# Weight splits and running sums on VectorE instead of GpSimd, and another order of the recurrence

## The chip, the cores and the metric

The kernel runs on one core of one Trainium2 chip. A core has five engines that run their own instruction rows in order and meet at semaphores: TensorE (PE, matrix products; PEld is its weight load), VectorE (DVE), ScalarE (ACT), GpSimd (POOL) and SyncE (SP, which here only issues DMAs). Matrix products write to PSUM; all else lies in SBUF. The metric is the device time of one execution in microseconds (us).

## What is computed

A two-layer network on 512 latent and 256 context tokens of width 1024. Layer 0 mixes tokens by a gated linear recurrence (RG-LRU), layer 1 by attention with compressed keys (MLA); each layer ends in a SwiGLU feed-forward (FFN). Every half of a layer normalises, shifts and scales its input by a modulation that depends on the conditioning vector, and adds its result, gated, to the residual. The part that the change touches most, cut down:

```python
def _rglru_coeffs(xc, gw, gb, lam):
    r = sigmoid(_blockdiag(xc, gw[0]) + gb[0])
    ig = sigmoid(_blockdiag(xc, gw[1]) + gb[1])
    log_a = -RG_C * r * softplus(-lam)
    return exp(log_a), sqrt(-expm1(2.0 * log_a)) * (ig * xc)

def _rglru_mixer(h_ctx, h_lat, ...):
    g, u = split(h @ w_in, 2)            # latent and context
    u = _dwconv_centred(u, conv_w, conv_b)
    for d, reverse in enumerate((False, True)):
        a, b = _rglru_coeffs(u, gate_w[d], gate_b[d], lam[d])
        y[d] = _linear_scan(a, b, h0, reverse)
    return ((y[0] + y[1]) * gelu(g)) @ w_out

def _rmsnorm(x, g):
    return x * rsqrt(mean(x * x, axis=-1) + NORM_EPS) * g
```

## The kernel before, in words

The residual xT lies transposed in SBUF: 8 tiles (m or k, 0 to 7) of 128 channels by 768 tokens, context behind the 512 latents. All products are in fp32 precision, made of three products of split numbers: a high half (wh, hh, uh, mh) and a low half (wl, hl, ul, ml), `mm3`: high by high, high by low, low by high. So each weight tile is split on the chip. SP loads a raw buffer (two of them), ACT writes the high half (L108), and `Stream._low` writes the low half, raw minus high (L119), on the engine that `low_engine` names: GpSimd at first, VectorE from the boundary ahead of FFN 0 on (`st.low_engine = dve`, L1061), GpSimd again for FFN 0's last boundary, and in later stages as MLA and FFN 1 set it. A split is 128x1024 in most cases. `advance` writes the high half of a unit and leaves its low half pending; the low half is written by the next `advance` or `flush`, so on the engine that does it the split stands behind all that was given to that engine in between. Writing the last low half of a raw buffer releases it, and SP's next load goes out. Four split tiles are held at a time.

The recurrence has four blocks n of 256 channels, and the list STEPS sets the order of everything in it by hand. A step is a letter and digits: `g` and `u` are the two input products of a block (48 matmul instructions each), `c` its convolution (L895 on ACT, six L899 on DVE, then the split L904 on ACT and L905 on DVE), `t` and `T` a gate product with its tanh (L931 on ACT), `e` the decay (L941 and L951 on DVE, L948 to L950 on ACT), `q` a root (L1037), `s` the states (L956, scans L958 and L959 or L962, L964 on DVE), `G` a GELU (L970), `m` the gated states and their split (L985 to L988), `o` one output product (12 matmul instructions) with its residual (L767 on DVE), `a` a step of the modulation of later stages, and `w` hands back a used weight tile, which is where `advance` is called. Three PSUM tiles go round among the products. The first digit is the block, the last of an `o` is m. START sets the order of the stage ahead of it in the same way: `H` is a flush, `B` and `D` transposes of rows of constants, `p` a product of the first input unit, `n` and `l` the normalisation.

`residual` adds an output product to xT (L767), squares the new xT on ACT (L783) and adds the square to a running sum (L785), on GpSimd, 52 times in the kernel. The addition is put off: it is written behind the L767 of the next m. In `boundary`, which writes the last half of a stage's output products and interleaves the next stage's normalisation (L669 and L672 on DVE, L671 on ACT), `flush_acc()` writes it at once for every m from the one on at which the first half's normalisation begins.

Of the kernel before, what the change touches and what calls it, by code (L numbers as in the profile page):

```python
# [12 lines left out]
ALU = mybir.AluOpType  # L13
# [3 lines left out]
D = 1024  # L17
# [20 lines left out]
START = (  # L38
    "H h0 L1 S00 X S01 S02 Y B S03 E0 h1 n0 l0 n1 h2 D S10 H l1 S11 S12 p01 S13 p00 L2 p10 E1 p11 n2 "
    "l2 S20 p02 p12 C S21 n3 S22 S23 l3 p20 p21 E2 n4 p22 p31 p30 l4 p32 n5 L3 S30 l5 A S31 S32 S33 "  # L40
# [21 lines left out]
class Stream:  # L62
# [3 lines left out]
    def __init__(self, nc, raw_pool, w_pool):  # L66
        self.nc, self.raw_pool, self.w_pool = nc, raw_pool, w_pool
        self.loads, self.units = [], []
        self.loaded = self.split = self.base = 0
        self.raw, self.tiles, self.freed, self.pending = {}, {}, set(), []  # L70
        self.hold = 0
        self.more = {}
        self.low_engine = nc.gpsimd

# [71 lines left out]
def kernel(ctx, tc, x, c, ctx_in, c_ctx, ada_w, ada_b, norm_mix_g, norm_ffn_g, ffn_w_in,  # L146
# [3 lines left out]
    nc = tc.nc  # L150
    act, dve, pe = nc.scalar, nc.vector, nc.tensor
# [109 lines left out]
    st = Stream(nc, raw_pool, w_pool)  # L261
# [23 lines left out]
    def lru_gate_unit(n, d):  # L285
# [18 lines left out]
        "a g31 s311 w o20 o21 G30 o22 G31 w m3 w o23 o24 o25 o26 o27").split()  # L304

# [458 lines left out]
    def residual(m, ps, l, ch, group, stat):  # L764
# [5 lines left out]
        if stat:  # L770
# [5 lines left out]
            else:  # L776
# [7 lines left out]
                if not at_end:  # L784
                    accs.append(lambda: nc.gpsimd.tensor_tensor(acc[:, s], acc[:, s], sq, op=ALU.add))  # L785

# [349 lines left out]
    def ffn0(na, nb, nxt):  # L1136
        ga, gb = na.group, nb.group
        with ExitStack() as es:
# [163 lines left out]
            for c, (h0, nh, outs) in enumerate(s0_out):  # L1302
# [3 lines left out]
                if lastp:  # L1306
                    ada_until(1, 4)
                    for m in range(KT):
                        ps = out_tile(c, m, (ga,), range(nh))
                        residual(m, lambda s: ps[1], 0, 5, ga, True)  # L1310
                        if m == 0:
                            st.flush()
                    st.low_engine = nc.gpsimd

                    def last(m):
# [440 lines left out]
```

## Time and profile before

| | us |
|---|---|
| median of 3 runs | 1568.83 |
| lowest, highest | 1565.91, 1569.62 |
| the profiled execution | 1571.79 |
| its span in the trace | 1569.9 |

| engine | busy us | share of the span |
|---|---|---|
| PE | 1512.2 | 96% |
| DVE | 934.2 | 60% |
| ACT | 675.9 | 43% |
| POOL | 281.5 | 18% |

Stages in the span: the start to some 48 us, the recurrence to 340, the mixer's last half and the boundary to 376, FFN 0 to 893, its boundary to 915, MLA to 1182, FFN 1 behind it. A share of busy time is a mean over stages; what bounds a stage is read from its windows and from the waits in it.

### The profile page before, as it was taken

The numbers are of one execution on the slowest core, as the hardware profiler recorded it, in microseconds if no ns is written. First come the engines' busy times: TensorE is split into PE (matmuls) and PEld (weight loads), VectorE is DVE, ScalarE is ACT, GpSimd is POOL, SyncE is SP. The second block draws the span as 40 slices with busy tenths as digits, with TensorE's granted clock in tenths as the row PEclk, the third lists the DMA queues.
The fourth block names the chain that finished last, engine by engine and source line by source line (L and its number), as shares of the span: only waits on it lengthen the run. The fifth ranks groups of instructions, "written<-read, shape, count | busy, mean of one in ns | idle before, by whom it ended". The sixth has DMA issues, their size and how long they took to land.

```text
span 1569.9 us, 21629 instructions
## 1 busy us (share of the span) xinstructions
PE 1512.2 (96%) x8903; PEld 1321.4 (84%) x8903; DVE 934.2 (60%) x1397; ACT 675.9 (43%) x989; POOL 281.5 (18%) x261
## 2 busy tenths in 40 slices
PE   7999998979999999999999998999998999999998
PEld 5877876868878898999989887899998888888887
DVE  5766778686855657767587457666537543233234
ACT  5486555734423241433424343766644322232223
POOL 3223333242010101001010332111144100000002
PEclk9999999989999999999999999999999999999999
DMA  9434333131233334333242112110112433223222
GB/s 359 127 108 135 108 122 120 59 103 48 68 108 114 104 112 128 114 114 122 94 141 64 51 56 69 29 43 28 54 54 75 161 118 104 81 98 117 81 69 93
DMA packets 134995, 155.14 MB, mean 99 GB/s; under 512 B 6252, under 2 KB 112353, under 8 KB 134897
## 3 DMA queue, kind: packets, MB, share of 16 engines
q1 hardware_dynamic: 122272, 112.21, 22.3%
q0 software_dynamic: 12320, 41.02, 8.2%
q8 instruction: 70, 1.15, 0.3%
q10 hardware_dynamic: 304, 0.53, 0.1%
q14 instruction: 29, 0.23, 0.0%
HBM read 151.64 MB, written 2.10 MB: 98 GB/s over the span
## 4 chain that ended last, share of the span: by engine, by line
PE 82%; DVE 11%; ACT 4%; issue 1%; DMA 1%; SPq 0%; POOL 0%; DVEq 0%; ACTq 0%; POOLq 0%
PE f L791 14%; PE fo L1212 11%; PE x L1166 10%; PE fo L791 8%; PE z L1166 5%; PE lo L791 3%; PE s L1555 3%; PE ga L791 2%; PE wo L791 2%; PE y L1166 2%; PE o L1597 2%; PE p L791 2%; PE g L791 2%; DVE yc L899 1%; PE t L1573 1%
## 5 line engine op out<-in xcount | busy, mean ns | idle before, releaser
L108 ACT ACTIVATE wh<-raw 128x1024 fp32r<-128x1024 f32 (+3 forms) x247 | 208.5, 871 | 203.9 <-PE fo L1212 64.5
L119 POOL TENSOR_TENSOR wl<-raw,wh 128x1024 fp32r<-128x1024 f32 (+3 forms) x66 | 157.5, 2397 | 328.8 <-ACT wh L108 328.6
L119 DVE TENSOR_TENSOR wl<-raw,wh 128x1024 fp32r<-128x1024 f32 (+2 forms) x181 | 169.3, 948 | 11.8 <-ACT wh L108 11.8
L767 DVE SCALAR_TENSOR_TENSOR xT<-fo,mod,xT 128x512 f32<-128x512 f32 (+1 forms) x124 | 74.1, 626 | 129.8 <-PE fo L1212 66.2
L239 POOL DMA_DIRECT2D ada<-in_ada_w_dram x96 | 51.7, 539 | 465.3 <-PE psada L570 217.9
L791 PE MATMUL f<-hh,wh 128*128 128x512 f32 x320 | 124.7, 390 | 0.0
L791 PE MATMUL f<-hh,wl 128*128 128x512 f32 x320 | 124.5, 389 | 0.0
L791 PE MATMUL f<-hl,wh 128*128 128x512 f32 x320 | 124.5, 389 | 0.0
L785 POOL TENSOR_TENSOR acc<-acc,sq 128x256 f32<-128x256 f32 (+1 forms) x52 | 50.7, 975 | 374.1 <-ACT sq L783 371.9
L1212 PE MATMUL fo<-ah,wh 128*128 128x512 f32 (+1 forms) x352 | 98.3, 345 | 0.9 <-DVE g L1273 0.8
L1212 PE MATMUL fo<-al,wh 128*128 128x512 f32 (+1 forms) x352 | 95.8, 338 | 0.4 <-DVE al L1201 0.4
L1212 PE MATMUL fo<-ah,wl 128*128 128x512 f32 (+1 forms) x352 | 95.3, 337 | 0.0
L1109 DVE TENSOR_TENSOR sg<-sg,f 128x512 f32<-128x512 f32 x20 | 13.7, 687 | 116.4 <-ACT sg L1108 116.4
L1108 ACT ACTIVATE sg<-f 128x512 f32<-128x512 f32 x20 | 12.0, 599 | 148.3 <-PE f L791 148.3
L791 PE MATMUL fo<-ah,wh 128*128 128x512 f32 (+1 forms) x200 | 73.0, 365 | 0.0
L791 PE MATMUL fo<-ah,wl 128*128 128x512 f32 (+1 forms) x200 | 72.7, 364 | 0.0
L791 PE MATMUL fo<-al,wh 128*128 128x512 f32 (+1 forms) x200 | 72.7, 364 | 0.0
L791 PEld LDWEIGHTS f<-hh,wh 128*128 128x128 f32 x320 | 60.1, 188 | 13.2 <-issue 0.8
L791 PEld LDWEIGHTS f<-hh,wl 128*128 128x128 f32 x320 | 60.1, 188 | 12.6
L791 PEld LDWEIGHTS f<-hl,wh 128*128 128x128 f32 x320 | 60.1, 188 | 12.4
L1212 PEld LDWEIGHTS fo<-ah,wh 128*128 128x128 f32 x352 | 56.2, 188 | 12.8 <-issue 4.6
L1212 PEld LDWEIGHTS fo<-al,wh 128*128 128x128 f32 x352 | 56.2, 188 | 8.0 <-DVE al L1201 0.7
(490 smaller groups left out, 4023.3 us busy)
## 6 DMA issues: line engine op xcount, KB each, us to landing
raw<-in_ffn_w_in_dram SPq DMA_DIRECT2D x26, 1024.0 KB, 4.9
ada<-in_ada_w_dram POOLq DMA_DIRECT2D x96, 256.0 KB, 3.1
raw<-in_ffn_w_out_dram SPq DMA_DIRECT2D x19, 1024.0 KB, 4.9
raw<-in_ffn_w_in_dram SPq DMA_DIRECT2D x36, 512.0 KB, 4.7
ada<-in_ada_w_dram POOLq DMA_DIRECT2D x30, 512.0 KB, 4.4
ada<-in_ada_w_dram SPq DMA_DIRECT2D x32, 256.0 KB, 5.5
raw<-in_lru_w_in_dram SPq DMA_DIRECT2D x10, 512.0 KB, 5.3
raw<-in_lru_gate_w_dram SPq DMA_DIRECT2D x16, 256.0 KB, 3.2
```

What stands on the lines that cost most here:

```text
L108: nc.scalar.activation(dst(hi), src(self.raw[load]), AF.Copy)
L119: self.low_engine.tensor_tensor(dst(lo), src(self.raw[load]), dst(hi).bitcast(F32), op=ALU.subtract)
L239: eng.dma_start(t, ada_w[l, k * P:(k + 1) * P, c0:c0 + 512])
L767: dve.scalar_tensor_tensor(xT[:, m, s], ps(s) if callable(ps) else ps[:, s], mod[:, l, ch, v, m:m + 1], xT[:, m, s], op0=ALU.mult, op1=ALU ...
L785: accs.append(lambda: nc.gpsimd.tensor_tensor(acc[:, s], acc[:, s], sq, op=ALU.add))
L791: pe.matmul(ps[:, off + s.start:off + s.stop], a, b[:, s], start=first and i == 0, stop=last and i == 2)
L899: dve.scalar_tensor_tensor(y[:, s0:s1], ps[:, s0 + o:s1 + o], convw(tap, k), y[:, s0:s1], op0=ALU.mult, op1=ALU.add)
L1166: pe.matmul(ps, w[:, o:o + P], x[:, k0 + k, s], start=first and k == 0 and q == 0, stop=last and k == 3 and q == 2, skip_group_check=not f ...
L1212: pe.matmul(ps[v], w[:, o:o + P], x[:, k, s], start=k == 0 and q == 0, stop=k == nh - 1 and q == 2)
L1555: pe.matmul(ps[:, o:o + 384], x, y[:, k0:k1], start=j == 0, stop=j == 4)
L1573: pe.transpose(ps[:, j * P:(j + 1) * P], prs[h, b][:, j // 3, j % 3 * P:(j % 3 + 1) * P], ident)
L1597: pe.matmul(ps[:, :256], x[:, t % 4, hs], y[:, t, :], start=t == 0 and j == 0, stop=t == NT - 1 and j == 2)
```

## The change

It does four things. `low_engine` is VectorE from the start, and the line that set it to GpSimd ahead of FFN 0's last boundary is gone; MLA and FFN 1 set it as before. The addition in `residual` is on VectorE. START has one flush more and the two first products of p exchanged. STEPS has another order: c11 ahead of s011, o10 behind t201, and block 2's last output products (o20 to o27) between the last gates, decays and states of block 3. GpSimd is left with 27 of its 66 splits and none of its 52 additions.

```diff
--- before.py
+++ after.py
@@ -36,7 +36,7 @@
 ENTRY_AT = (12, 6)
 
 START = (
-    "H h0 L1 S00 X S01 S02 Y B S03 E0 h1 n0 l0 n1 h2 D S10 H l1 S11 S12 p01 S13 p00 L2 p10 E1 p11 n2 "
+    "H h0 L1 S00 X S01 S02 Y H B S03 E0 h1 n0 l0 n1 h2 D S10 H l1 S11 S12 p00 S13 p01 L2 p10 E1 p11 n2 "
     "l2 S20 p02 p12 C S21 n3 S22 S23 l3 p20 p21 E2 n4 p22 p31 p30 l4 p32 n5 L3 S30 l5 A S31 S32 S33 "
     "p41 E3 n6 p40 l6 p42 p52 p51 p61 n7 p50 l7 C p60 p70 h3 p71 p62 p72 H C").split()
 
@@ -70,7 +70,7 @@
         self.raw, self.tiles, self.freed, self.pending = {}, {}, set(), []
         self.hold = 0
         self.more = {}
-        self.low_engine = nc.gpsimd
+        self.low_engine = nc.vector
 
     def load(self, cols, emit):
         self.loads.append([cols, emit, 0])
@@ -295,13 +295,13 @@
 
     STEPS = (
         "g01 a t000 w G01 T000 t001 w e000 T001 a g10 e001 G10 a q000 s000 q001 a t011 t010 w s001 a T010 "
-        "e010 T011 e011 u10 q010 w a a s010 q011 c10 u11 w s011 a a w g11 c11 t100 w T100 m0 G11 w a a "
+        "e010 T011 e011 u10 q010 w a a s010 q011 c10 u11 w c11 s011 a a w g11 t100 w T100 m0 G11 w a a "
         "t101 e100 T101 e101 q101 g20 q100 G20 w a o00 t110 T110 t111 T111 w a a s101 s100 o01 o02 e111 "
         "o03 o04 o05 o06 q111 e110 w s111 o07 w a u20 c20 a a q110 s110 w w u21 c21 g21 m1 a a t200 G21 "
-        "T200 o10 w e200 t201 a o11 T201 o12 o13 e201 w q200 a q201 s201 w s200 a t210 T210 a t211 T211 "
+        "T200 w e200 t201 o10 a o11 T201 o12 o13 e201 w q200 a q201 s201 w s200 a t210 T210 a t211 T211 "
         "e211 w u30 e210 c30 q210 w o14 o15 q211 s210 a a s211 w u31 c31 o16 a w o17 a t301 t300 m2 T300 "
-        "e300 T301 e301 a t310 w T310 t311 a e310 a T311 e311 q300 q310 q311 g30 q301 s300 s310 s301 w w "
-        "a g31 s311 w o20 o21 G30 o22 G31 w m3 w o23 o24 o25 o26 o27").split()
+        "e300 T301 e301 a t310 w T310 t311 a e310 T311 o20 o21 a e311 q300 q310 o22 q311 w o23 g30 q301 s300 a "
+        "w s310 G30 w o24 s301 o25 g31 s311 G31 o26 w m3 o27 w").split()
 
     g_units[0][0], = std_units(lru_w_in[0], 0, P)
     u_units[0] = [std_units(lru_w_in[0], D + i * P, P)[0] for i in range(2)]
@@ -782,7 +782,7 @@
                     sq = sq[:, :s.stop - s.start]
                 act.activation(sq, xT[:, m, s], AF.Square)
                 if not at_end:
-                    accs.append(lambda: nc.gpsimd.tensor_tensor(acc[:, s], acc[:, s], sq, op=ALU.add))
+                    accs.append(lambda: dve.tensor_tensor(acc[:, s], acc[:, s], sq, op=ALU.add))
 
     def mm3(ps, wh, wl, xh, xl, parts, first, last, off=0):
 
@@ -1310,8 +1310,6 @@
                         residual(m, lambda s: ps[1], 0, 5, ga, True)
                         if m == 0:
                             st.flush()
-                    st.low_engine = nc.gpsimd
-
                     def last(m):
                         ps = out_tile(c, m, (gb,), range(nh))
                         residual(m, lambda s: ps[0], 0, 5, gb, True)
```

DVE around the first output product that reads the second output unit of block 1, o14 (lo_4_2297). yc is a convolution, ul the low half of its result, tg and b are parts of gates and decays, wl the low half of a weight unit; before:

```order
L941 SCALAR_TENSOR_TENSOR tg_2167<-tg_2167,yc_1786 128x768
L951 SCALAR_TENSOR_TENSOR tg_2152<-b_2272,tg_2152 128x768
L899 SCALAR_TENSOR_TENSOR yc_2277<-u_0_2221,cols_d,yc_2277 128x511 x2
L899 SCALAR_TENSOR_TENSOR yc_2277<-u_0_2221,cols_d,yc_2277 128x510
L899 SCALAR_TENSOR_TENSOR yc_2277<-u_0_2221,cols_d,yc_2277 128x255 x2
L899 SCALAR_TENSOR_TENSOR yc_2277<-u_0_2221,cols_d,yc_2277 128x254
L905 TENSOR_TENSOR ul_2286<-yc_2277,uh_2285 128x768
L767 SCALAR_TENSOR_TENSOR xT<-lo_4_2297,mod,xT 128x512
```

and now:

```order
L941 SCALAR_TENSOR_TENSOR tg_2167<-tg_2167,yc_1786 128x768
L951 SCALAR_TENSOR_TENSOR tg_2152<-b_2272,tg_2152 128x768
L899 SCALAR_TENSOR_TENSOR yc_2277<-u_0_2221,cols_d,yc_2277 128x511 x2
L899 SCALAR_TENSOR_TENSOR yc_2277<-u_0_2221,cols_d,yc_2277 128x510
L899 SCALAR_TENSOR_TENSOR yc_2277<-u_0_2221,cols_d,yc_2277 128x255 x2
L899 SCALAR_TENSOR_TENSOR yc_2277<-u_0_2221,cols_d,yc_2277 128x254
L905 TENSOR_TENSOR ul_2286<-yc_2277,uh_2285 128x768
L119 TENSOR_TENSOR wl_2219<-raw_2110,wh_2218 128x1024
L767 SCALAR_TENSOR_TENSOR xT<-lo_4_2297,mod,xT 128x512
```

The split wl_2219 stands between ul and the residual of lo_4; before it was on POOL's row.

DVE around block 3's last decay, ahead of the products g30 and g31, before:

```order
L941 SCALAR_TENSOR_TENSOR tg_2540<-tg_2540,yc_2402 128x768
L951 SCALAR_TENSOR_TENSOR tg_2480<-b_2544,tg_2480 128x768
L941 SCALAR_TENSOR_TENSOR tg_2589<-tg_2589,yc_2277 128x768
L951 SCALAR_TENSOR_TENSOR tg_2568<-b_2614,tg_2568 128x768
L941 SCALAR_TENSOR_TENSOR tg_2636<-tg_2636,yc_2402 128x768
L951 SCALAR_TENSOR_TENSOR tg_2604<-b_2640,tg_2604 128x768
L956 TENSOR_TENSOR tg_2495<-tg_2495,tg_2518 128x768
L958 SCALAR_TENSOR_TENSOR tg_2495<-a_2521,tg_2495 128x256
L959 SCALAR_TENSOR_TENSOR tg_2495<-a_2521,tg_2495 128x512
```

and now:

```order
L941 SCALAR_TENSOR_TENSOR tg_2589<-tg_2589,yc_2277 128x768
L951 SCALAR_TENSOR_TENSOR tg_2568<-b_2614,tg_2568 128x768
L767 SCALAR_TENSOR_TENSOR xT<-lo_0_2634,mod,xT 128x512
L767 SCALAR_TENSOR_TENSOR xT<-lo_0_2634,mod,xT 128x256
L767 SCALAR_TENSOR_TENSOR xT<-lo_1_2649,mod,xT 128x512
L767 SCALAR_TENSOR_TENSOR xT<-lo_1_2649,mod,xT 128x256
L941 SCALAR_TENSOR_TENSOR tg_2632<-tg_2632,yc_2402 128x768
L951 SCALAR_TENSOR_TENSOR tg_2604<-b_2670,tg_2604 128x768
L767 SCALAR_TENSOR_TENSOR xT<-lo_2_2677,mod,xT 128x512
L767 SCALAR_TENSOR_TENSOR xT<-lo_2_2677,mod,xT 128x256
L119 TENSOR_TENSOR wl_2574<-raw_2441,wh_2573 128x1024
L767 SCALAR_TENSOR_TENSOR xT<-lo_3_2699,mod,xT 128x512
```

Three output products stand among the decays, and the split wl_2574, which g30 reads, stands behind the decay of tg_2604 and the residual of lo_2.

DVE in the last half of the mixer, ahead of FFN 0 (sq is ACT's square, nt and hl are the normalised input), before:

```order
L669 SCALAR_TENSOR_TENSOR nt_2_512_3101<-xT,gm,R_f0a 128x256
L672 SCALAR_TENSOR_TENSOR hl_79<-nt_1_512_3086,mod,hh_78 128x256
L767 SCALAR_TENSOR_TENSOR xT<-lo_5_3105,mod,xT 128x512
L669 SCALAR_TENSOR_TENSOR nt_3_512_3116<-xT,gm,R_f0a 128x256
L672 SCALAR_TENSOR_TENSOR hl_79<-nt_2_512_3101,mod,hh_78 128x256
L767 SCALAR_TENSOR_TENSOR xT<-lo_6_3120,mod,xT 128x512
L669 SCALAR_TENSOR_TENSOR nt_4_512_3131<-xT,gm,R_f0a 128x256
L672 SCALAR_TENSOR_TENSOR hl_79<-nt_3_512_3116,mod,hh_78 128x256
L767 SCALAR_TENSOR_TENSOR xT<-lo_7_3135,mod,xT 128x512
```

and now:

```order
L767 SCALAR_TENSOR_TENSOR xT<-lo_3_3072,mod,xT 128x512
L785 TENSOR_TENSOR acc<-acc,sq_3080 128x512
L669 SCALAR_TENSOR_TENSOR nt_1_512_3086<-xT,gm,R_f0a 128x256
L672 SCALAR_TENSOR_TENSOR hl_79<-nt_0_512_3069,mod,hh_78 128x256
L767 SCALAR_TENSOR_TENSOR xT<-lo_4_3090,mod,xT 128x512
L785 TENSOR_TENSOR acc<-acc,sq_3098 128x512
L669 SCALAR_TENSOR_TENSOR nt_2_512_3101<-xT,gm,R_f0a 128x256
L672 SCALAR_TENSOR_TENSOR hl_79<-nt_1_512_3086,mod,hh_78 128x256
L767 SCALAR_TENSOR_TENSOR xT<-lo_5_3105,mod,xT 128x512
L785 TENSOR_TENSOR acc<-acc,sq_3113 128x512
L669 SCALAR_TENSOR_TENSOR nt_3_512_3116<-xT,gm,R_f0a 128x256
L672 SCALAR_TENSOR_TENSOR hl_79<-nt_2_512_3101,mod,hh_78 128x256
```

Each L767 is followed by the addition of its own square.

## Rows read from the trace of the kernel before

**Rows 1.** The page, part 1: busy us of each engine.

```profile
PE 1512.2 (96%) x8903; PEld 1321.4 (84%) x8903; DVE 934.2 (60%) x1397; ACT 675.9 (43%) x989; POOL 281.5 (18%) x261
```

**Rows 2.** Windows: busy us of each engine, instruction counts, PE's granted clock, DMA.

```profile
300.00:350.00 50.00, 41.58 (x238) 35.71 (x237) 38.39 (x47) 24.00 (x33) 21.72 (x13) 0.90 0.26 84
...
376.00:860.00 484.00, 482.74 (x2906) 438.60 (x2905) 325.31 (x526) 169.70 (x288) 41.42 (x77) 1.00 0.34 103
```

**Rows 3.** Waits of PE, 100 to 352 us: total, times, longest in us.

```profile
PE lo L791 <- DVE xT L767: 8.2, 1, 8.2
...
PE ga L791 <- DVE yc L899: 5.1, 1, 5.1
...
PE ga L791 <- ACT tg L931: 1.4, 1, 1.4
...
PE lo L791 <- ACT tg L931: 3.0, 1, 3.0
...
PE ga L791 <- ACT uh L904: 3.0, 1, 3.0
```

**Rows 4.** Windows, one stretch after the wait for L767.

```profile
326.20:332.20 6.00, 6.00 (x19) 5.13 (x20) 5.96 (x9) 3.07 (x4) 0.35 (x1) 0.50 0.01 3
```

**Rows 5.** Timeline of PE (start us, duration, instruction): the last gate's end.

```profile
293.30 0.51 PE L791 MATMUL ga<-ul,wh 128*128 128x512 f32 x2
293.65 0.53 PE L791 MATMUL ga<-uh,wl 128*128 128x512 f32 x2
```

**Rows 6.** Groups (xcount, busy us, mean ns, idle before), 48 to 352 us, and timeline rows.

```profile
L119 POOL TENSOR_TENSOR wl<-raw,wh 128x1024 fp32r<-128x1024 f32 x31 | 82.4, 2661 | 101.1 <-ACT wh L108 100.8
...
L964 DVE TENSOR_TENSOR tg<-tg,tg 128x768 f32<-128x768 f32 x8 | 18.4, 2297 | 0.3
...
108.71 2.53 POOL L119 TENSOR_TENSOR wl<-raw,wh 128x1024 fp32r<-128x1024 f32 x1
...
109.08 2.98 DVE L964 TENSOR_TENSOR tg<-tg,tg 128x768 f32<-128x768 f32 x1
...
261.81 0.96 DVE L964 TENSOR_TENSOR tg<-tg,tg 128x768 f32<-128x768 f32 x1
```

**Rows 7.** Timeline of DVE: a split with no neighbour on POOL.

```profile
366.45 1.22 DVE L119 TENSOR_TENSOR wl<-raw,wh 128x1024 fp32r<-128x1024 f32 x1
```

**Rows 8.** Timeline of all engines around block 3's first convolution, c30.

```profile
245.03 3.12 POOL L119 TENSOR_TENSOR wl<-raw,wh 128x1024 fp32r<-128x1024 f32 x1 [6.85 <-ACT wh L108]
...
248.23 0.99 ACT L895 ACTIVATE yc<-u,cols_d 128x768 f32<-128x768 f32 x1 [0.37 <-PE u L791]
...
249.25 3.75 DVE L899 SCALAR_TENSOR_TENSOR yc<-u,cols_d,yc 128x511 f32<-128x511 f32 x6 [0.30 <-ACT yc L895]
...
253.97 0.96 DVE L905 TENSOR_TENSOR ul<-yc,uh 128x768 fp32r<-128x768 f32 x1 [0.97 <-ACT uh L904]
```

**Rows 9.** Timeline of DVE: the last decay of block 3.

```profile
303.57 0.96 DVE L951 SCALAR_TENSOR_TENSOR tg<-b,tg 128x768 f32<-128x768 f32 x1 [3.08 <-ACT tg L950]
```

**Rows 10.** Timeline of DVE: diagonals in the start and ahead of FFN 0.

```profile
15.17 3.06 DVE L855 TENSOR_SCALAR dgx<-ident,rst 128x128 f32<-128x128 f32 x6
...
368.23 0.88 DVE L656 TENSOR_SCALAR dg_f0b<-ident,rst 128x128 f32<-128x128 f32 x4
```

**Rows 11.** Timeline of DVE and ACT in the boundary ahead of FFN 0.

```profile
342.14 0.48 DVE L767 SCALAR_TENSOR_TENSOR xT<-lo,mod,xT 128x256 f32<-128x256 f32 x1 [0.24 <-PE lo L791]
...
356.92 0.74 DVE L767 SCALAR_TENSOR_TENSOR xT<-lo,mod,xT 128x512 f32<-128x512 f32 x1
...
358.65 0.74 DVE L767 SCALAR_TENSOR_TENSOR xT<-lo,mod,xT 128x512 f32<-128x512 f32 x1
...
360.76 1.88 DVE L119 TENSOR_TENSOR wl<-raw,wh 128x1024 fp32r<-128x1024 f32 x1
...
357.75 0.63 ACT L783 ACTIVATE sq<-xT 128x512 f32<-128x512 f32 x1 [0.35 <-DVE xT L767]
```

**Rows 12.** Groups of DVE in the boundary after FFN 0, 890 to 915 us.

```profile
L672 DVE SCALAR_TENSOR_TENSOR hl<-nt,mod,hh 128x256 fp32r<-128x256 f32 x6 | 6.8, 1130 | 2.1 <-ACT hh L671 2.1
```

## The prediction, made blind

> **What bounds the kernel now.** I read the page first: TensorE (PE) is busy for 96% of the span [rows 1], so a change can gain only from the time in which PE stands still or runs at a low clock, and can lose wherever PE is made to wait. The windows by stage say where such time is [rows 2]: in 376 to 860, layer 0's feed-forward product, PE is busy 482.74 of 484.00 us, and what VectorE (DVE) and GpSimd (POOL) do there costs nothing. In 300 to 350, the end of the recurrence, it is busy 41.58 of 50.00. The waits of PE between 100 and 352 us name the releasers [rows 3]: 8.2 us for DVE's L767, 5.1 for DVE's convolution (L899), 3.0 and 1.4 for ScalarE's (ACT) gate tanh (L931), 3.0 for the high half of the convolved input (L904). That is 20.7 us. After a wait comes a stretch in which the granted clock is 0.50 of full speed, that is 1.2 GHz: 326.20 to 332.20 follows the 8.2 us wait [rows 4]. Pairs of products start 0.35 us apart at full speed (293.30 and 293.65, [rows 5]) and, over these 6.00 us with 19 products in them, about 0.63 apart, so a slow stretch loses some 0.45 of its length. I call these slow stretches the tail of a wait.
>
> **The splits, moved from POOL to DVE.** 31 weight splits fall in 48 to 352 us and take 2661 ns each on POOL [rows 6]; the same 128x1024 split on DVE takes 1.22 us at 366.45 [rows 7]. POOL also slows DVE: L964 takes 2.98 us at 109.08, beside the split that starts at 108.71, and 0.96 at 261.81 with none beside it; its eight have a mean of 2297 ns [rows 6]. The eight alone lose 8 x (2.30 - 0.96) = 10.7 us, and I estimate some 40 us for all of DVE's instructions in this stretch, from the same comparison form by form. 31 x 1.22 = 38 us of splits come in. So DVE's load stays about as it is, and what matters is where each split stands in its row.
>
> The Trainium skill ("GPSIMD Engine Reference", section "8. Key points") says that elementwise work is about twice as fast on VectorE and that GpSimd shares its SBUF interfaces with VectorE instructions that have two SBUF inputs. The trace agrees: 2661 against 1220 ns, and 2.98 against 0.96. By this rule alone the change would gain; that is the first rival below, whose time is worked out from rows.
>
> On POOL a split starts when ACT has written the high half; nothing else stands ahead of it but some DMA issues. DVE takes its instructions in order, and the low half of a unit is written at the next step that advances the weights, behind all that DVE was given in between. Where one of these waits for ACT or PE, the split waits, and PE stops at the third product of the unit, the first that reads the low half. The largest case: output unit o14. Before, POOL made its split at 245.03 [rows 8]. Now it stands behind block 3's convolution and its L905. PE ends the u product at about 248.23, when ACT starts on it, the convolution runs from 249.25 for 3.75 us, L905 starts at 253.97 and takes 0.96, and a split of 1.22 follows: 253.97 + 0.96 + 1.22 = 256.15 [rows 7, 8]. PE would have wanted it at 248.23 + 2 x 0.35 + some 0.1 for the start. So about 7.1 us are lost, and a tail that I take like the one in [rows 4], 0.45 x 6.0 = 2.7: together 9.8.
>
> The second: g30. Its split now stands behind L951 of e311 and two L767. Before, the last gate's products ended at 293.65 + 0.53 = 294.2 [rows 5], and that L951 at 303.57 + 0.96 = 304.5 [rows 9]: 10.3 us later. Now PE has four output products (o20 to o23, six pairs each, 6 x 0.35 = 2.1 us) and one step of the modulation (some 0.6) ahead of g30, 9.0 us, and reaches the low half at 9.7. The split is done at 10.3 + 0.75 + 0.48 + 1.22 = 12.7. That is 3.0 lost, and a tail of 0.45 x 3.4 = 1.5 (a short one: between nothing and 2.7): 4.5.
>
> Walking the rest of the recurrence the same way (durations of the rows, the new order of each engine), I get these further new waits, all estimates: t000, 1.25 (its low half waits for two splits); t100, 1.25 (a split behind the first states); u20, 0.8; g21, 2.4 (behind a convolution and a state); T201, 1.2 (its tanh behind a decay on ACT); t210, 2.6 (behind L767 and a decay); t301, 2.0 (what stays of the wait for the last convolution, which starts when o14's loss is over); the first product of the mixer's last half, 2.5. Their sum is 14.0. With the two large ones it is 28.3.
>
> **The reordered steps.** Convolution c11 ahead of states s011 takes away the wait for L904, 3.0. The later o10 lets PE go on where it waited 3.0 and 1.4 for L931. The wait of 5.1 for c31's convolution goes, since DVE is late with it by the slowed L962 and L964 ahead of it (its rest is the t301 above). The output products among block 3's last gates take the 8.2 us wait away: L767 is no longer queued up behind all states. That is all of [rows 3], 20.7, and four tails of about 3.4, 3.4, 4.7 and 6.0 us, 0.45 x 17.5 = 7.9. Sum: 28.6. So the recurrence comes out at 28.3 - 28.6, about -0.3: the two halves of the edit cancel. I bound it by -20 and +12: the first if only o14's wait appears with its tail (9.8 - 28.6), the second if three of the waits over 2 us get a long tail too and c31's wait stays.
>
> **The start** (POOL beside DVE): the six dgx of the first normalisation take 3.06 us at 15.17 beside a split, where four of the like take 0.88 at 368.23 without a neighbour [rows 10]: 3.06 - 6 x 0.22 = 1.7 goes, and as much again, as an estimate, where two L669 of the same chain meet a split at 23.8. Two splits on DVE take 2 x 1.22 = 2.4 back, some 0.5 of it beside other waits. I put -1.5, between -3 and 0. The order of p00 and p01 and the extra flush change nothing else.
>
> **The sums of squares, moved to DVE.** This is an addition ahead of nothing in the feed-forwards, but in the boundaries between stages DVE is what PE waits for. From the second product of the last half on, the addition stands right behind the same m's L767 and so waits for ACT's square of it. In the rows of before, L767 starts at 356.92 and the next at 358.65, 1.73 apart; the square starts at 357.75 and ends at 358.38 [rows 11]. So the addition can start 358.38 - 356.92 = 1.46 after its L767, takes about 0.65 (an L767 of the same size, 0.74, overlapped as its neighbours are), and then come the normalisation's two (L669, L672) at 0.4 each: 2.9 from L767 to L767. Six m of 2.9 - 1.7 are 7.2; the split that POOL slowed to 1.88 us at 360.76 [rows 11] runs at its 1.22, and its neighbours too, some -1.2: +6. In the half ahead of it L767 comes every 0.72 us (0.48 and an idle of 0.24, [rows 11]); with an addition of 0.48 DVE needs 0.96, 7 x 0.24 = 1.7, and two of the last splits, 2.4, now lie on it: +4. PE waits for the last of this chain, so all of it counts: +10, between +5 and +12. After it, FFN 0 is full and gives nothing back.
>
> From FFN 0 to MLA the same loop runs with a slower PE (some 2.7 us per m), and POOL's splits slow L672 there to a mean of 1130 ns [rows 12], where an L767 of its size takes 0.48 [rows 11]; that goes: six m of 2.9, splits of 2 x 1.22 + 2 x 0.69 and a rest of 2 are 23.5 against 21 before: +3 with the start (0 to +5). From MLA to FFN 1, in halves of 256, the splits stay on POOL, and each of eight m gains a wait of about 0.3 and an addition of 0.48, 6.2 in all, less what L672 gets back when POOL's additions are gone, eight times up to 0.65 (the excess in [rows 12]), of which I take 4.2: +2 (0 to +4). At the end of FFN 1 PE needs as long for an m as DVE would: 0.
>
> **Sum.** -1.5 - 0.3 + 10 + 3 + 2 = +13.2 us. The profiled execution took 1571.8 us, 3.0 above the median of 1568.8; on its frame the sum gives 1585.0, on the median's 1582.0, which I take.
>
> **Rivals.** *Faster: POOL's neighbourhood was the real brake.* If DVE's freed time (40 us) comes at the instants where a split is due, the new waits stay at o14's alone: 9.8 - 28.6 = -19 in the recurrence, -3 at the start, and boundaries at their low end, +5: -17, or 1552. For it: DVE is free for 11.6 of the 50 us of 300 to 350 [rows 2], and L962 and L964 stand in the way of c31 and of the last L767. Against it: the splits' places behind waiting instructions are fixed by the order. It decides from a recurrence better by 13 us on. *No change*: a recurrence better by 10 to 16 us, and boundaries at +10 to +15; some 1564 to 1573. *Slower still*: tails behind every new wait over 2 us, and the raw buffers, released by the split, come free so late that the next DMA is awaited too; +12 in the recurrence, +19 in the boundaries, 1597. For it: two raw buffers only.
>
> **How the numbers follow.** My forecast, slower by 4 to 20 us, has 0.52; slower still 0.08; no change 0.14; faster 0.26. This measurement can tell about 0.3%, 4.7 us, from no change. The forecast's own range is 1573 to 1589. The range that should hold 8 in 10 goes from 1556, which takes in half of the faster case, to 1597. Faster 0.26, same 0.14, slower 0.60.
>
> **What would show it.** A wait of PE of about 7 us at o14's third product, released by DVE's L119, and shorter ones at g21, t210 and g30; no wait for L767 in the recurrence above 3 us; L964 and L962 at 0.96 and 1.76 us throughout; in the boundary ahead of FFN 0 L767 every 2.9 us, and DVE's idle there ended by ACT's L783; FFN 0's start 7 to 10 us later. I am wrong if FFN 0 starts earlier than before, or if L785 on DVE finds its square done.

## The result and the profile after

The changed kernel takes 1586.51 us (median of 4 runs, 1582.47 to 1590.04) beside 1569.22 for the kernel before, run with it: a ratio of 1.0113, with a 95% interval of 1.0083 to 1.0144. That is 17.7 us slower, 13.0 to 22.6 by the interval. The profiled execution took 1590.04 us, its span is 1588.3, 18.4 more than the span before. The page, part 1, answers to [rows 1]:

```profile
PE 1521.0 (96%) x8903; PEld 1326.1 (83%) x8903; DVE 947.9 (60%) x1488; ACT 678.3 (43%) x989; POOL 131.6 (8%) x170
```

POOL has lost 150 us of work and DVE has gained 14. Where the 18.4 us arose is read from the start times of the same product in both traces (a step of 2 or 3 us between two single traces can be chance, see the last section):

| first product of | before | after | later by, us | of it in this stage | predicted |
|---|---|---|---|---|---|
| the first gate (end of the start) | 70.18 | 70.32 | 0.1 | +0.1 | -1.5 |
| the mixer's last half (end of the recurrence) | 339.7 | 340.8 | 1.1 | +1.0 | -0.3 |
| f00u, FFN 0 | 369.36 | 380.29 | 10.9 | +9.8 | +10 |
| cst_kv, MLA | 944.37 | 957.75 | 13.4 | +2.5 | +3 |
| cst_f1b, FFN 1 | 1198.55 | 1215.49 | 16.9 | +3.5 | +2 |
| cst_fina, the end | 1552.21 | 1570.57 | 18.4 | +1.5 | 0 |

The recurrence's waits, 50 to 320 us (total, times, longest), in place of those of [rows 3]:

```profile
PE lo L791 <- DVE wl L119: 7.2, 1, 7.2
PE g L791 <- DVE wl L119: 5.4, 2, 2.9
PE ga L791 <- ACT tg L931: 3.7, 3, 1.6
PE ga L791 <- DVE wl L119: 3.4, 2, 2.2
PE u L791 <- DVE wl L119: 0.5, 1, 0.5
```

None of the old releasers but the gate's tanh is left; L119, the split, releases 16.5 of the 20.5 us of waits in this stretch. At o14 DVE does what the prediction's sum said, 2.8 us later than in [rows 8] since the recurrence is late by that much there. The columns are start, duration, instruction and, in brackets, idle time and its releaser:

```profile
252.09 3.75 DVE L899 SCALAR_TENSOR_TENSOR yc<-u,cols_d,yc 128x511 f32<-128x511 f32 x6 [0.85 <-ACT yc L895]
256.81 0.96 DVE L905 TENSOR_TENSOR ul<-yc,uh 128x768 fp32r<-128x768 f32 x1 [0.97 <-ACT uh L904]
257.68 1.22 DVE L119 TENSOR_TENSOR wl<-raw,wh 128x1024 fp32r<-128x1024 f32 x1
```

```profile
258.95 1.01 PE L791 MATMUL lo<-mh,wl 128*128 128x512 f32 x2 [7.23 <-DVE wl L119]
```

The split ends at 258.90, and PE, which has done two pairs, goes on at 258.95 after 7.23 us. The window behind it (granted clock: the number ahead of the last two) is the tail:

```profile
259.00:264.00 5.00, 5.00 (x16) 4.29 (x17) 1.14 (x2) 2.66 (x3) 0.00 (x0) 0.53 0.35 105
```

DVE itself has been relieved as expected. Its groups from 48 to 300 us (count, busy us, mean ns), to be set against [rows 6]: L964 takes 958 ns in the mean instead of 2297, and a split 1217 ns instead of 2661.

```profile
L119 DVE TENSOR_TENSOR wl<-raw,wh 128x1024 fp32r<-128x1024 f32 x24 | 29.0, 1217 | 5.7 <-ACT wh L108 5.7
...
L964 DVE TENSOR_TENSOR tg<-tg,tg 128x768 f32<-128x768 f32 x6 | 5.7, 958 | 0.2
```

In the boundary ahead of FFN 0 ([rows 11] before), DVE:

```profile
361.43 0.74 DVE L767 SCALAR_TENSOR_TENSOR xT<-lo,mod,xT 128x512 f32<-128x512 f32 x1
362.93 0.69 DVE L785 TENSOR_TENSOR acc<-acc,sq 128x512 f32<-128x512 f32 x1 [0.76 <-ACT sq L783]
363.54 0.47 DVE L669 SCALAR_TENSOR_TENSOR nt<-xT,gm,R_f0a 128x256 f32<-128x256 f32 x1
363.93 0.48 DVE L672 SCALAR_TENSOR_TENSOR hl<-nt,mod,hh 128x256 fp32r<-128x256 f32 x1
364.33 0.74 DVE L767 SCALAR_TENSOR_TENSOR xT<-lo,mod,xT 128x512 f32<-128x512 f32 x1
```

From one L767 to the next it is 2.90 us (361.43 to 364.33), and DVE stands 0.76 us idle in front of each addition until ACT's square is there.

### The profile page after: what moved, and what is told of

The parts are those of the page before. It is cut to its first block, busy times and chain, and to the rows that moved or that the text cites. A ratio compares the mean times of both kernels' runs of the same rounds, so it can differ in the third digit from the quotient of the medians.

```text
span 1588.3 us, 21561 instructions
## 1 busy us (share of the span) xinstructions
PE 1521.0 (96%) x8903; PEld 1326.1 (83%) x8903; DVE 947.9 (60%) x1488; ACT 678.3 (43%) x989; POOL 131.6 (8%) x170
## 4 chain that ended last, share of the span: by engine, by line
PE 81%; DVE 10%; ACT 5%; DMA 2%; issue 1%; SPq 1%; DVEq 0%; ACTq 0%
PE f L791 14%; PE fo L1212 11%; PE x L1166 9%; PE fo L791 8%; PE z L1166 5%; PE s L1553 3%; PE u L791 3%; PE lo L791 2%; PE y L1166 2%; PE wo L791 2%; PE g L791 2%; PE o L1595 2%; PE ga L791 2%; DVE yc L899 2%; PE t L1571 1%; DVE wl L119 1%
## 5 line engine op out<-in xcount | busy, mean ns | idle before, releaser
L119 DVE TENSOR_TENSOR wl<-raw,wh 128x1024 fp32r<-128x1024 f32 (+2 forms) x220 | 214.2, 986 | 23.7 <-ACT wh L108 23.5
L767 DVE SCALAR_TENSOR_TENSOR xT<-fo,mod,xT 128x512 f32<-128x512 f32 (+1 forms) x124 | 74.1, 626 | 123.0 <-PE fo L791 62.3
L119 POOL TENSOR_TENSOR wl<-raw,wh 128x1024 fp32r<-128x1024 f32 (+2 forms) x27 | 57.9, 2163 | 325.6 <-ACT wh L108 325.6
L791 PEld LDWEIGHTS f<-hh,wh 128*128 128x128 f32 x320 | 60.1, 188 | 13.3 <-issue 0.8
L1212 PEld LDWEIGHTS fo<-ah,wh 128*128 128x128 f32 x352 | 56.9, 190 | 12.8 <-issue 4.6
L1212 PEld LDWEIGHTS fo<-ah,wl 128*128 128x128 f32 x352 | 57.0, 190 | 7.8
```

The lines of the kernel that those rows point to most:

```text
L119: self.low_engine.tensor_tensor(dst(lo), src(self.raw[load]), dst(hi).bitcast(F32), op=ALU.subtract)
L767: dve.scalar_tensor_tensor(xT[:, m, s], ps(s) if callable(ps) else ps[:, s], mod[:, l, ch, v, m:m + 1], xT[:, m, s], op0=ALU.mult, op1=ALU ...
L791: pe.matmul(ps[:, off + s.start:off + s.stop], a, b[:, s], start=first and i == 0, stop=last and i == 2)
L1212: pe.matmul(ps[v], w[:, o:o + P], x[:, k, s], start=k == 0 and q == 0, stop=k == nh - 1 and q == 2)
```

## The experiments

The change has three separable parts: splits (S) and additions (A), each on GpSimd (P) or VectorE (D), and the order. Four of the six mixed kernels were run, so that with before and after the table of ratios to the kernel before (95% interval) is full up to two:

| order | S on P, A on P | S on P, A on D | S on D, A on P | S on D, A on D |
|---|---|---|---|---|
| of before | 1 | 1.0078 (1.0053 to 1.0103) | 1.0101 (1.0072 to 1.0129) | not run |
| changed | 1.0011 (0.9999 to 1.0023) | not run | 1.0046 (1.0025 to 1.0067) | 1.0113 (1.0083 to 1.0144) |

Differences between two of these ratios are given in us below; their own intervals are some 4 to 6 us either way, as both ratios have one.

**The order alone.** The edit is the START and STEPS of the change on the kernel before.

> Before's engines for splits and additions, the changed order of START and STEPS alone. Theory A (the order by itself removes the waits for L904, L931, c31's convolution and L767, and only the splits on VectorE bring new waits): FFN 0 starts 8 to 20 us earlier than before and the time is 1550 to 1561 us. Theory B (the new order only works together with splits on VectorE, since the slowed scans and the doubled split time on GpSimd come due earlier in it): within 5 us of before, 1564 to 1574, or slower.

Measured: a ratio of 1.0011, no change. Theory B holds for the sum. The waits of PE, 50 to 340 us, say a part of why:

```profile
PE g L791 <- DVE xT L767: 5.3, 1, 5.3
PE ga L791 <- ACT tg L931: 4.3, 2, 3.0
PE ga L791 <- DVE yc L899: 2.3, 1, 2.3
```

The wait for L904 is gone, as is the one of 8.2 us for L767 in front of an output product, but a wait of 5.3 us for L767 stands in front of a g product now, and those for L931 stay. The rest is behind the recurrence: the first product of the mixer's last half starts 6.4 us earlier than before (333.30 against 339.70), but cst_f0a, the sum over its squares, only 3.2 earlier (345.50 against 348.69). What the order gained in the recurrence it half paid back there; the rest of this trace's gain does not show in the ratio.

**Splits on VectorE in the order of before.** The edit:

```diff
-        self.low_engine = nc.gpsimd
+        self.low_engine = nc.vector
...
-                    st.low_engine = nc.gpsimd
-
                     def last(m):
```

> The kernel before with only the splits moved to VectorE, in the order of before. Theory A (a split waits behind whatever waits ahead of it on VectorE, and the order of before keeps its own waits for the convolutions): new waits of some 20 us in the recurrence against a relief of 5 to 12 us in c31 and L767, +4 in the boundary ahead of FFN 0: 8 to 20 us slower, 1577 to 1589. Theory B (relief from GpSimd's neighbourhood outweighs): 1555 to 1567.

Measured: 1.0101, 15.8 us slower: theory A. Its waits for the split, 50 to 340 us:

```profile
PE g L791 <- DVE wl L119: 12.4, 2, 10.0
PE lo L791 <- DVE wl L119: 7.2, 1, 7.2
```

The longest in front of a g product is 10.0 us, where the changed order has 2.9, and the wait for L904, which the changed order does not have, is 4.3 us here and 3.0 before.

**The change with the additions back on GpSimd**, and **the kernel before with only the additions on VectorE.** The edits are this line, in either direction:

```diff
-                    accs.append(lambda: dve.tensor_tensor(acc[:, s], acc[:, s], sq, op=ALU.add))
+                    accs.append(lambda: nc.gpsimd.tensor_tensor(acc[:, s], acc[:, s], sq, op=ALU.add))
```

> The changed kernel with only the 52 additions back on GpSimd. Theory A (behind L767 each addition waits for its square and so stretches the boundaries): 9 to 13 us faster than the changed kernel, 1574 to 1578 us, with L767 in the boundary ahead of FFN 0 back at some 1.75 us apart, and what is left is about +4 from the last splits on VectorE there and +2 elsewhere. Theory B (the boundaries lose time because VectorE is simply too full, splits above all): under 5 us faster, 1582 to 1587.

> The kernel before with only the additions moved to VectorE. Theory A: the boundaries lose what they lose in the changed kernel less the splits: +5 to +6 ahead of FFN 0, +2 to +3 after it, +3 ahead of FFN 1, +1 at the end, in all 11 to 14 us slower than before, 1580 to 1583, and nothing in the recurrence. Theory B: under 6 us slower, since GpSimd's additions no longer slow VectorE's normalisation.

Measured: 1.0046 and 1.0078. The additions cost (1.0113 - 1.0046) x 1569 = 10.5 us in the changed kernel, and 0.0078 x 1569 = 12.2 us in the kernel before: theory A in both, by the time. The splits cost 15.8 us in the old order and (1.0046 - 1.0011) x 1569 = 5.5 us in the new one. So the new order is worth (1.0101 - 1.0046) x 1569 = 8.6 us where splits are on VectorE and nothing where they are not.

Where the three parts cost ahead of FFN 0 is seen in the start times of three products in each trace. The first part runs from the first product of the mixer's last half to cst_f0a, the second from there to f00u:

| kernel | first part, us | second part, us |
|---|---|---|
| before | 9.0 | 20.7 |
| only the additions on VectorE | 8.7 | 24.8 |
| only the splits on VectorE | 12.8 | 22.2 |
| only the order | 12.2 | 20.8 |
| splits and order | 14.7 | 21.7 |
| the change | 14.9 | 24.6 |

In both pairs that differ by them, the additions lengthen the second part alone, by 3 to 4 us; the first part is lengthened by the splits and by the order. Theory A for the kernel with only the additions put 5 to 6 us ahead of FFN 0 and 3 ahead of FFN 1; its trace shows 3.8 and 4.5.

**The additions put off by one m.** The edit, on the changed kernel:

```diff
             if i >= i1:
-                flush_acc()
+                if i == n - 1:
+                    flush_acc()
```

> The changed kernel; in the boundaries each addition is put off to behind the next m's L767, as in the other loops, where its square is done. Theory A (the price of the additions in the boundaries is mainly the wait for the square, 0.76 us per m on an idle VectorE): L767 ahead of FFN 0 comes every 2.2 to 2.4 us instead of 2.9, and the three boundaries give back 3 + 2 + 2 us: 5 to 8 faster than the changed kernel, 1578 to 1582. Theory B (the price is the addition's own 0.69 us and the fuller engine): under 2 us faster, 1585 or more.

Measured: 1.0091 (1.0070 to 1.0111), 3.5 us faster than the changed kernel by the ratios. It lies between the two theories, and with both intervals (some 6 us either way) it decides for neither, nor does it show a gain. In DVE's timeline (its lines lie one further down, L768 is the L767 of the others) the wait for the square is gone:

```profile
363.59 0.74 DVE L768 SCALAR_TENSOR_TENSOR xT<-lo,mod,xT 128x512 f32<-128x512 f32 x1
364.25 0.68 DVE L786 TENSOR_TENSOR acc<-acc,sq 128x512 f32<-128x512 f32 x1
...
365.63 0.74 DVE L768 SCALAR_TENSOR_TENSOR xT<-lo,mod,xT 128x512 f32<-128x512 f32 x1
```

An L767 follows its forerunner after 2.04 us instead of 2.90, less than the 2.2 to 2.4 of theory A. But FFN 0's f00u starts at 380.43, where it started at 380.29. The slow stretch there is longer now: behind 2.27 us of waiting from 371.4 on, the granted clock is 0.50 over

```profile
373.50:383.50 10.00, 9.85 (x46) 9.85 (x47) 4.68 (x13) 1.46 (x4) 0.00 (x0) 0.50 0.31 105
```

in which PE was busy for 9.85 of 10.00 us. In the changed kernel the slow stretch of this place lay at 369.5 to 376.4, where PE was busy for 5.1 of 6.9 us only. Behind FFN 0, the boundaries gave back 2.9 us and 0.4, the end 1.1 (from the same landmarks as above). So the wait for the square is shown, but not that it is what the additions' 10.5 us consist of: ahead of FFN 1, where they cost 3.6 us in the traces with and without them, putting them off gave back 0.4.

**One flush ahead of o14's convolution.** The edit, on the changed kernel, with an op `h` that calls `st.flush()`:

```diff
-        "e211 w u30 e210 c30 q210 w o14 o15 ...
+        "e211 w u30 h e210 c30 q210 w o14 o15 ...
```

> The changed kernel with one flush ahead of e210, so that the low half that o14 reads is made ahead of the convolution c30 instead of behind it. Both theories expect that the wait of 7.2 us at o14 goes. Theory A (the wait is mostly paid for the later wait for c31's convolution, which it hides): that one comes back with 3 to 5 us, and the time is 2 to 6 us below the changed kernel, 1581 to 1585. Theory B (the wait and its slow stretch are a loss of their own): 9 to 10 us faster, 1577.

Measured: 1.0057 (1.0037 to 1.0078), 8.8 us faster than the changed kernel. Theory B is the nearer one. Of its waits, 50 to 320 us,

```profile
PE g L791 <- DVE wl L119: 5.3, 2, 2.8
...
PE ga L791 <- DVE yc L899: 1.4, 1, 1.4
```

the 7.2 us at o14 are gone and c31's convolution (L899) costs 1.4 us, where the kernel before waited 5.1 [rows 3]. It doesn't come back at its old size: L962 and L964 ahead of it take 1758 and 958 ns in the mean, the latter 2297 before [rows 6].

**Flushes at five places**, in the changed order with splits on VectorE and additions on GpSimd. The edits in STEPS (each `h` is new):

```diff
+   c11 h s011 ... u21 h c21 g21 ... w e200 t201 h o10 ... u30 h e210 c30 ... a e310 h T311 o20
```

> Splits on VectorE in the changed order, additions on GpSimd, and a flush at five places of the recurrence, so that the low halves for t100, g21, t210, o14 and g30 are made ahead of the convolution, decay or state that they stood behind. Theory A (the splits cost by their place alone, 5.6 us against the same order with GpSimd): the waits for L119 between 100 and 320 us, 16 us in sum, fall under 5, and the recurrence ends 3 to 8 us earlier than without the flushes: 1569 to 1574. Theory B (VectorE is too full for 31 more splits, wherever they stand): the same waits come back at L767, L899 or L931, and the time stays at 1575 to 1579.

Measured: 0.9934 (0.9914 to 0.9954), 1559.80 us: 17.6 us faster than without the flushes, and faster than the kernel before. Theory A has the direction, and the gain is more than twice what it put. PE's waits, 50 to 320 us:

```profile
PE ga L791 <- ACT tg L931: 3.7, 3, 1.8
PE g L791 <- DVE wl L119: 2.5, 1, 2.5
PE ga L791 <- DVE yc L899: 1.4, 1, 1.4
```

**c11 ahead of s011 as the only edit on the kernel before.**

```diff
-  u11 w s011 a a w g11 c11 t100
+  u11 w c11 s011 a a w g11 t100
```

> The kernel before with one exchange: c11 ahead of s011. Theory A (this exchange takes away the wait of 3.0 us for L904, 0.4 for L905 and the slow stretch behind them, and nothing later takes it back): 4 to 5 us faster than before, 1564 to 1565. Theory B (the chain on VectorE or ScalarE later in the recurrence sets its end, and what is gained here is lost at T201, c31 or the last L767): within 2 us of before.

Measured: 0.9963 (0.9948 to 0.9978), 5.8 us faster: theory A, with a little more than it put, and its wait of 5.1 us for c31's convolution is 2.3. The rest of the new order thus costs (1.0011 - 0.9963) x 1569 = 7.5 us on GpSimd's splits.

**The five flushes with the other steps in the order of before, splits on VectorE.** The edit, on the kernel before with the splits on VectorE:

```diff
-  u11 w s011 a a w g11 c11 t100
+  u11 w c11 h s011 a a w g11 t100
+  ... u21 h c21 g21 ... w e200 t201 h a o11 ... u30 h e210 c30 ... a e310 h a T311
```

> Splits on VectorE, additions on GpSimd, the order of before with c11 ahead of s011 and the same five flushes: against the early-flush kernel in the changed order, only o10 and o20 to o27 stand where they stood before. Theory A (with splits made early, the gain is the relief of VectorE and not the order, and the two orders are worth the same): within 4 us of the early-flush kernel, 1557 to 1564. Theory B (the output products among block 3's last gates are worth 5 to 10 us once the splits are early, since in the order of before L767 queues up behind all the states and PE waits 8 us for it): 1565 to 1571.

Measured: 0.9937 (0.9914 to 0.9960), as in the changed order: the time is theory A's. Its reason, the relief of VectorE, is tested next.

**The same, with the splits back on GpSimd.** This kernel differs from the kernel before by c11's exchange and the five flushes alone; against the last one:

```diff
-        self.low_engine = nc.vector
+        self.low_engine = nc.gpsimd
...
+                    st.low_engine = nc.gpsimd
+
                     def last(m):
```

> The kernel before with c11 ahead of s011 and the five flushes, splits and additions on GpSimd as before. Theory A (the flushes matter only on VectorE, where something stands ahead of the split; what the early-flush kernels have over c11's exchange is the relief of VectorE from GpSimd's splits): as the kernel with the exchange alone, 1562 to 1566. Theory B (earlier low halves and earlier raw buffers are the gain, on either engine): 1556 to 1561.

Measured: 0.9940 (0.9918 to 0.9963), 1558.80 us. Theory B is nearer: with the splits made early the kernel is as fast with GpSimd as with VectorE. My explanation, that the relief of VectorE makes the gain, falls. Over c11's exchange alone (0.9963) the flushes give 3.6 us here, about as much as the two intervals can tell. What changed is seen at 201 to 209 us. Before, POOL's timeline reads

```profile
205.24 1.10 POOL L242 DMA_DIRECT2D ada<-in_ada_w_dram  x2 [6.40 <-PE psada L570]
206.36 2.42 POOL L119 TENSOR_TENSOR wl<-raw,wh 128x1024 fp32r<-128x1024 f32 x1
```

and DVE's

```profile
205.16 4.44 DVE L985 TENSOR_TENSOR gel<-tg,gel 128x768 f32<-128x768 f32 x2
```

The split stands behind two DMA issues, which wait for PE's modulation step, and so it falls beside the two L985, which take 4.44 us. The gated states that follow are late, ACT's tanh behind them too, and PE waits 3.0 us for it ([rows 3], L931). With the flush, POOL has done the split by 198.5, beside a convolution that reads PSUM,

```profile
191.46 7.02 POOL L119 TENSOR_TENSOR wl<-raw,wh 128x1024 fp32r<-128x1024 f32 x2 [4.56 <-ACT wh L108]
201.80 1.09 POOL L242 DMA_DIRECT2D ada<-in_ada_w_dram  x2 [3.32 <-PE psada L570]
```

which takes 3.74 us all the same, and the two L985 take 1.82 in DVE's timeline:

```profile
196.13 3.74 DVE L899 SCALAR_TENSOR_TENSOR yc<-u,cols_d,yc 128x511 f32<-128x511 f32 x6
...
201.72 1.82 DVE L985 TENSOR_TENSOR gel<-tg,gel 128x768 f32<-128x768 f32 x2
```

PE's waits, 50 to 340 us, show the wait for L931 in front of an output product at 0.4, and the one for L767 as it was:

```profile
PE lo L791 <- DVE xT L767: 8.3, 1, 8.3
...
PE lo L791 <- ACT tg L931: 0.4, 1, 0.4
```

It is the flushes and not the exchange that do this: in the kernel with c11's exchange alone, the wait and the slow L985 stand as before.

```profile
PE lo L791 <- ACT tg L931: 3.0, 1, 3.0
```

```profile
202.51 4.43 DVE L985 TENSOR_TENSOR gel<-tg,gel 128x768 f32<-128x768 f32 x2
```

So on GpSimd a split waits too, for the issues ahead of it, and its place decides which of DVE's instructions it slows.

**The last two splits ahead of FFN 0 on GpSimd**, on the early-flush kernel in the changed order:

```diff
+    st.flush()
+    st.low_engine = nc.gpsimd
     for i in used:
         st.done(i)
```

> The early-flush kernel (splits on VectorE, additions on GpSimd, changed order) with the last two splits ahead of FFN 0, those of FFN 0's first units, on GpSimd. Theory A (in the first half of the mixer's last products VectorE is the bound, and two splits of 1.22 us there cost what they take and a part of the 2.1 us wait for L767): 3 to 5 us faster, 1555 to 1557. Theory B (on GpSimd they slow L767, L985 and L988 by as much, or FFN 0's first product then waits for them): within 2 us, 1558 to 1562.

Measured: 0.9945 (0.9928 to 0.9963): no gain, theory B. The wait for L767 that was 2.1 us is gone, and another has taken its place, since the additions on GpSimd now stand behind the splits (waits of PE, 320 to 360 us):

```profile
PE cst_f0a L648 <- POOL acc L785: 2.2, 1, 2.2
```

**The change as made, with the five flushes alone.** The edit, on the changed kernel:

```diff
+   c11 h s011 ... u21 h c21 g21 ... w e200 t201 h o10 ... u30 h e210 c30 ... a e310 h T311 o20
```

> The changed kernel with the five flushes alone, additions still on VectorE. Theory A (the place of the splits and the additions cost apart from each other: 17 us by the flushes where the additions were on GpSimd, 9.8 us by the additions): 1568 to 1571 us, that is no slower than before. Theory B (the additions hide behind waits that the flushes take away, or the other way round): 1573 to 1580.

Measured: 1.0019 (1.0007 to 1.0032), 3 us slower than before and 14.7 faster than the changed kernel: close to theory A (1571.97 us, a little above the range that it put), in which splits and additions cost apart from each other. (1.0019 - 0.9934) x 1569 = 13.3 us is what the additions cost here.

## Why the prediction was right, and where it was not

The forecast, slower by 13 us with a range of 1556 to 1597, held: 1586.5, slower by 17.7. Of its mechanism, the half on the splits held place by place; the half on the additions has the right sign, but its largest term, +10 ahead of FFN 0, came out by luck.

- *Splits wait behind what stands ahead of them on VectorE.* Right at the places named: o14 7.2 us (put at 7.1), g30 2.9 (3.0), g21 2.5 (2.4), t210 2.2 (2.6), t100 1.2 (1.25), u20 0.5 (0.8). The runs with flushes show the cause: a flush moves only the split, and with it the release of its raw buffer, and 14.7 to 17.6 us go.
- *The recurrence cancels.* Put at -0.3, it was +1.0, a small difference of two sums of 28, in which errors met. t000 and t301 have no wait for a split (1.25 and 2.0 put). Against that, T201 waits 1.6 (1.2 put), the 3.0 for L931 at o10, which I struck off, is left with 1.6 in front of t201, which stands in o10's place, and g21's wait has a slow stretch (198.87 to 202.28) for which I had put none.
- *The additions wait for their square.* The loop is as put, 2.90 us from L767 to L767 (2.9), and 2.04 with the wait taken away. Not as put is what it costs. I put the +10 ahead of FFN 0 together from 6 by this loop, 1.7 by the additions ahead of it and 2.4 by two splits, so 7.7 by additions. By the table of parts, additions make 3 to 4 of the 9.8 and nothing in the first part; splits and order make the other 6.8, most of it in the first part. There three splits stand among the first L767, not two, and two slow stretches lie (342.23 to 345.64 and 349.06 to 352.47, at 0.50). That the two errors met is luck. DVE in the first part:

```profile
343.55 1.22 DVE L119 TENSOR_TENSOR wl<-raw,wh 128x1024 fp32r<-128x1024 f32 x1
345.05 1.23 DVE L119 TENSOR_TENSOR wl<-raw,wh 128x1024 fp32r<-128x1024 f32 x1 [0.29 <-ACT wh L108]
...
346.34 0.47 DVE L767 SCALAR_TENSOR_TENSOR xT<-lo,mod,xT 128x256 f32<-128x256 f32 x1
346.73 1.21 DVE L119 TENSOR_TENSOR wl<-raw,wh 128x1024 fp32r<-128x1024 f32 x1
```

All additions together cost 10.5 and 12.2 us in the two factor pairs; how much of it is the wait for the square and how much the additions' own 0.69 us on a full engine stays open.

- *From FFN 0 to MLA*, put at +3, was +2.5, but some 1.5 of it, as an estimate, is a slow stretch late in FFN 0 (last section) that has nothing to do with this boundary.
- *The start*, put at -1.5: the relief came, the first product is 1.7 us earlier, and it was given back by the same mechanism, a split that I counted as "beside other waits". DVE, with ACT's high half late behind a DMA:

```profile
29.19 1.22 DVE L119 TENSOR_TENSOR wl<-raw,wh 128x1024 fp32r<-128x1024 f32 x1 [2.82 <-ACT wh L108]
30.33 1.14 DVE L672 SCALAR_TENSOR_TENSOR hl<-nt,mod,hh 128x512 fp32r<-128x512 f32 x2
```

It stood 2.82 us for the split, with the normalisation's L672 behind it, and PE waited 1.9 us for that.

- *From MLA to FFN 1*, put at +2, was +3.5, and *the end*, put at 0, +1.5. The additions alone explain the first: with them back on GpSimd the stage takes as long as before (254.2 us from cst_kv to cst_f1b in both traces, 257.7 in the changed kernel), so of the 4.2 us that I took back for L672, the trace leaves no more than 2.7, if the 6.2 ahead of them held. The waits in FFN 1's first half (before, 1.2 for L767 in front of f11g and none in front of f10g) and at the end:

```profile
PE f10g L791 <- DVE xT L767: 1.6, 1, 1.6
PE f11g L791 <- DVE xT L767: 1.5, 1, 1.5
```

```profile
PE cst_fina L648 <- DVE acc L785: 1.3, 1, 1.3
```

At the end I had compared rates per m and left out that the last addition must be done before the sum is taken: 1.3 us of waiting.

The Trainium skill ("GPSIMD Engine Reference", section "8. Key points") states that VectorE is about twice as fast at elementwise work and that GpSimd contends with VectorE instructions that have two SBUF inputs. The trace agrees in the durations, 1217 against 2661 ns for a split and 958 against 2297 for L964 without and with GpSimd's splits beside it; it doesn't say which way the kernel goes. The faster rival (26%) had one premise right, that VectorE's instructions would be relieved. The change could not use it, because the split's place in the row cost it 14.7 to 17.6 us. With that mended and the additions left where they were, the kernel is at 1559.8, 7.8 us above the rival's 1552, and the order of before (0.9937) and GpSimd (0.9940) do as well as that.

One sentence of the prediction is wrong in what it draws from "some DMA issues": that nothing much stands ahead of a split on GpSimd. The rows of POOL at 205 us of the kernel before, beside those of the kernel with the flushes and all splits on GpSimd, show 3 us of PE's time, and its tail, behind just that.

## What to carry to other kernels

When work moves to an engine that takes its instructions in order, ask for each piece what stands ahead of it there and what that waits for; here the same splits on VectorE made the kernel 15.8 us slower, and with five of them and one convolution a step earlier it was 9.9 us faster than before. The engine itself made no difference then: with the splits left on GpSimd the same steps gave 9.4 us. An accumulation behind an instruction of another engine costs a wait in each turn of the loop (0.76 us here); on GpSimd all additions were 10.5 us cheaper, while a turn later on VectorE gave no gain that these runs can tell from none. A slow neighbour costs by the instruction that it meets (two L985 took 4.44 us beside a split and 1.82 without it, the six L899 of a convolution 3.74 beside one and 3.75 in [rows 8]), so moving it in time can be worth as much as moving it to another engine. And a term that comes out as forecast is not yet a term understood: the +10 ahead of FFN 0 was made of other parts.

## What the runs showed of the hardware

The slow stretch after a wait does not come after each: behind the same wait of 2.2 us for the modulation late in FFN 0, the kernel before ran on at full clock, and others, among them the changed kernel and the one with the last two splits on GpSimd, fell to half. Windows of 3.2 us behind it, before first, then the changed kernel, then the other, the granted clock ahead of the last two numbers:

```profile
872.90:876.10 3.20, 3.18 (x27) 3.18 (x28) 2.51 (x7) 0.42 (x1) 0.00 (x0) 1.00 0.00 0
```

```profile
885.00:888.20 3.20, 3.20 (x17) 3.20 (x16) 1.61 (x2) 0.42 (x1) 0.00 (x0) 0.50 0.00 0
```

```profile
863.70:866.90 3.20, 3.20 (x17) 3.20 (x16) 1.24 (x6) 0.00 (x0) 0.00 (x0) 0.50 0.00 0
```

In these 3.2 us PE gets through 27 products or 17; a product starts 0.12 us after the last at the full clock and 0.21 at half, so such a stretch costs some 1.5 us, as an estimate. The kernel with the two splits on GpSimd was 2.7 us ahead of the early-flush kernel, whose clock did not fall there, at the end of the boundary and 0.4 ahead when MLA's cst_kv starts, with this stretch between. So a single difference of 2 or 3 us between two traces is no evidence of a gain; and a difference of two ratios has the interval given above. What decides whether the stretch comes was not found.
